# Where the differential attention's weights are scaled and split: in their own stage, or during the first MLP through DRAM

## The chip, the cores and the metric

One core of one Trainium2 chip runs the whole program. The metric is the device time of one execution in microseconds (us), the median of several runs.

## The reference

Two transformer blocks run one after the other on 512 tokens (16 meta tokens are put ahead, 528 columns in all) with a width of 1024. The first has two layers: a stick-breaking attention with a squared-ReLU MLP, and a differential attention with a second such MLP. The second block has a forgetting attention, a gated linear recurrence and a mixture of 32 experts. The change touches the second layer of the first block, cut here to its projections:

```python
h = h + squared_relu_mlp(h, mlp_norm_g[0], mlp_w_in[0], mlp_w_out[0])   # the first MLP
kvn = rmsnorm(h, kv_norm_g)
kv = kvn @ kv_w                                   # 1024 x 2048: keys and values
hn = rmsnorm(h, b_norm_g[j])
qq = (hn @ b_w_q[j])                              # 1024 x 1024: queries
o = differential_attention(q1, q2, k1, k2, vv, lam)
h = h + merge_heads(o) @ b_w_o[j]
h = h + squared_relu_mlp(h, mlp_norm_g[1], mlp_w_in[1], mlp_w_out[1])
```

`rmsnorm` divides by the root of the mean square and multiplies by a vector of gains; everything is float32. Since both norms see the same `h`, the kernel normalizes once and puts each norm's gains into the rows of the weight behind it.

## The kernel before, in words

A dense product is made at nearly float32 precision from three products of float32r: weight and activation are each split into a high part (a copy rounded to float32r) and a low part (the rest), and `product` (L164 on) adds high by high, high by low and low by high over eight blocks of 128 rows (L172 to L174). Weights come in column tiles of 128 x 8 x 128 (512 KB). A column tile is used on two halves of 264 columns, or on the 512 real ones. The result lies in one of two PSUM banks called `dn`, which VectorE evacuates (L202 in an MLP's second product, L367 in its first, L209 for attention's projections).

`sequence` (L76 on) lists all weight tiles of the program in the order in which they are used. `fetch` (L123) has up to NW = 3 raw tiles (`wraw`) on the way, loaded by SP's DMA queue. A tuple with a third entry names a norm: there GpSimd multiplies the raw tile by that norm's gains (L132). `take` (L135) keeps up to two split tiles ahead: ScalarE copies to `whi` (L144), VectorE subtracts to `wlo` (L145). Each of these names has two buffers.

The stages around the change, with the times of the profile:

- The first MLP (about 320 to 690 us), `mlp` (L355). Four rounds c: eight tiles of `mlp_in`, whose results are squared and split (`relu`, `rhi`, `rlo`), then eight tiles of `mlp_out` whose products are added to `h` (`accumulate`). In the last round each tile of `h` is also split for the next stage and stored to DRAM (`hbuf`, L643).
- The differential stage (about 690 to 945 us), `layer_b`. `df_dense` makes for head p the keys (tile `kv[p]`), the queries (`b_q[p]`) and the values (`kv[7 + p]`, one head later): 24 tiles. `head_norm` normalizes each head's keys and queries and rotates them, with a matmul (L703) and a GpSimd multiplication (L708); `stack` and `double` split them (L334, L335, L351 to L353). `df_attn` makes scores (L812), softmax (L825 to L869), transposes (L847), the product with the values (L919) and a norm of the output (L928, L314, L931).
- The output's weights `b_o` follow as raw tiles, then the second MLP with the same `mlp`.

TensorE's order is the program's: `script` steps through `df_attn`, and the tuples PAT, LEAD and END say by hand how many pieces of dense work go between two pieces of attention. The order on the other engines is set by a list scheduler in which evacuations and weight splits have a higher priority (AHEAD_E, AHEAD_W). Every engine works through its own queue in order.

```python
if len(n) > 2 and n[2] is not None:
    g = self.gains[:, n[2] * KT:(n[2] + 1) * KT]
    self.nc.gpsimd.tensor_mul(raw, raw, g[:, :, None].to_broadcast([128, KT, 128]))
```

Of the kernel before, what the change touches and what calls it, by code (L numbers as in the profile page):

```python
# [7 lines left out]
F32 = mybir.dt.float32  # L8
F32R = mybir.dt.float32r
# [8 lines left out]
KT = 8  # L18
# [4 lines left out]
HALVES = ((0, H0), (H0, L))  # L23
# [6 lines left out]
class Net:  # L30
    def __init__(self, ctx, tc, w):
        self.ctx, self.tc, self.nc, self.w = ctx, tc, tc.nc, w
        ctx.enter_context(tc.manual_schedule(engines={mybir.EngineType.PE}))
        self.const = ctx.enter_context(self.phase("const"))
        self.dense_pools = ExitStack()
        pools = self.dense_pools.enter_context
        self.wraw = ctx.enter_context(self.phase("wraw", self.NW, "right"))
        ctx.callback(self.dense_pools.close)
        self.act = pools(self.phase("act", 1, "right"))
        self.wsp = pools(self.phase("wsp", 2, "right"))  # L40
        self.dn = pools(self.banks("dn", 2, "right"))
        self.nc.scalar.preload_act_table_set("natural_log_exp_and_others")
        self.sources, self.rawq, self.splitq = iter(self.sequence()), [], []
        self.fetch(1)
        self.constants()

# [29 lines left out]
    def sequence(self):  # L76
        w = self.w
        for p in range(8):
            for i in range(3):
                yield w["a_qkv"][p, i], KT  # L80
        for k in range(2):
            for t in range(KT):
                yield w["a_o"][t][:, 4 * k:4 * k + 4, :], 4
        for layer in range(2):
            if layer:
                for p in range(9):
                    if p < 8:
                        yield w["kv"][p], KT, 2
                        yield w["b_q"][p], KT, 3
                    if p:  # L90
                        yield w["kv"][7 + p], KT, 2
                for k in range(2):
                    for t in range(KT):
                        yield w["b_o"][t][:, 4 * k:4 * k + 4, :], 4
            for c in range(4):
                for j in range(KT):
                    yield w["mlp_in%d" % layer][c * KT + j], KT
                for j in range(KT):
                    yield w["mlp_out%d" % layer][c, j], KT
        yield w["w2f"][0], KT  # L100
        for p in range(4):
            for c in (0, 4, 8):
                yield w["w2"][c + p], KT
        for h in range(8):
            for c in (20, 28, 12, 36):
                yield w["w2"][c + h], KT
        for t in range(2):
            yield w["w2"][44 + t], KT
            yield w["w2"][52 + t], KT
        for t in range(2):  # L110
            yield w["w_ao"][t], 4
        for t in range(KT):
            yield w["w_ho"][t], KT
            if t < 6:
                yield w["w2"][46 + t], KT
                yield w["w2"][54 + t], KT
                yield w["w_ao"][t + 2], 4
            if t < self.NWO:
                yield w["w_o"][t // 4, t % 4], KT, None, True
        for t in range(self.NWO, KT):  # L120
            yield w["w_o"][t // 4, t % 4], KT, None, True

    def fetch(self, most=8):  # L123
        while len(self.rawq) < min(most, self.NW):
            n = next(self.sources, None)
            if n is None:
                return
            raw = self.wraw.tile([128, KT, 128], F32, name="wraw")[:, :n[1], :]
            self.nc.sync.dma_start(raw, n[0])
            if len(n) > 2 and n[2] is not None:  # L130
                g = self.gains[:, n[2] * KT:(n[2] + 1) * KT]
                self.nc.gpsimd.tensor_mul(raw, raw, g[:, :, None].to_broadcast([128, KT, 128]))  # L132
            self.rawq.append((raw, len(n) > 3))

    def take(self):  # L135

        nc = self.nc
        while len(self.splitq) < 2 and self.rawq and not self.rawq[0][1]:
            raw, _ = self.rawq.pop(0)
            kt = raw.shape[1]  # L140
            hi = self.wsp.tile([128, KT, 128], F32R, name="whi")[:, :kt, :]
            lo = self.wsp.tile([128, KT, 128], F32R, name="wlo")[:, :kt, :]
            with self.tc.high_priority(offset=self.AHEAD_W):
                nc.scalar.activation(hi, raw, AF.Copy)  # L144
                nc.vector.tensor_sub(lo, raw, hi)  # L145
            self.splitq.append((hi, lo))
            self.fetch()
        return self.splitq.pop(0)
# [203 lines left out]
            self.nc.vector.tensor_sub(out[2 + i][r], x[r], out[i][r])  # L352
            self.nc.scalar.activation(out[i][self.ROWS[1 - i]], x[r], AF.Copy)  # L353

    def mlp(self, act, halves, after):  # L355
        nc = self.nc
        with self.phase("mlp") as mp, self.banks("mb", 1) as mb:
            extra = [mb.tile([128, 512], F32, name="mb%d" % i) for i in range(4)]
            for c in range(4):
                r = []  # L360
                for j in range(KT):
                    hi = mp.tile([128, L], F32R, name="rhi", bufs=12)
                    lo = mp.tile([128, L], F32R, name="rlo", bufs=12)

                    def sq(ps, a, b):
                        x = mp.tile([128, 512], F32, name="relu", bufs=3)[:, :b - a]
                        nc.vector.scalar_tensor_tensor(x, ps, 0.0, self.rstd[:, a:b], op0=ALU.max, op1=ALU.mult)  # L367
                        nc.scalar.activation(x, x, AF.Square, scale=0.5)
                        self.split(x, hi[:, a:b], lo[:, a:b])
                    if c == 0 and j < 2:  # L370
                        if j == 0:
                            ps = self.opening(act, halves, extra)
                            self.begin_norm()
                        else:
                            w = self.take()
                            ps = [self.product(w, act, a, b, x[:, :b - a]) for (a, b), x in zip(halves, extra[2:])]
                        for p, (a, b) in zip(ps, halves):
                            with self.tc.high_priority(offset=self.AHEAD_E):
                                sq(p, a, b)
                    else:  # L380
                        for _ in self.dense(act, sq, halves):
                            pass
                    r.append((hi, lo))
                self.accumulate(r, halves, after if c == 3 else None)

# [235 lines left out]
    def layer_a(self):  # L623
        self.hg = self.pair("hg", self.act)
        self.begin_norm()
        self.open_h(self.w["xT"], ALL)
        self.fetch()
        for t in range(KT):
            self.split_tile(t, self.h[:, t, :], [(0, self.hg, ALL)])
        for t in range(KT):  # L630
            self.square_tile(t, self.h[:, t, :])
        with self.phase("sbo") as op:
            o = self.pair("oT", op)
            with self.phase("sb") as self.ap, self.banks("zp", 4) as self.zp, self.banks("op", 1) as self.op:
                self.sb_setup()
                self.ready, self.used, self.outs, self.T, self.when = [], 0, 0, 0.0, []
                self.pace(self.sb_attn(o), self.sb_dense(self.hg2(), self.hg2(o)), self.RATIO_A)
            self.begin_norm()
            self.accumulate(self.hg2(o)[4:], HALVES, lambda t: self.norm_tile(t, self.h[:, t, :], [(1, self.hg, ALL)]))

        def after(t):
            self.norm_tile(t, self.h[:, t, :], [(None, self.hg, ALL)])
            self.nc.sync.dma_start(self.hbuf[:, t, :], self.h[:, t, :])  # L643
        self.mlp(self.hg2(), HALVES, after)
        self.hres.close()

    def hg2(self, pair=None):
# [1363 lines left out]
    PATH = (2, 2, 0, 0, 4, 2, 0, 0, 0, 0, 1, 0, 1)  # L2011

    def run(self):
        dram = self.ctx.enter_context(
            self.tc.tile_pool(name="hbuf", bufs=1, space=bass.MemoryType.DRAM))
        self.vbuf = dram.tile([S, D], F32, name="vbuf")
        self.hbuf, self.hrow = dram.tile([128, KT, L], F32, name="hbuf"), dram.tile([128, 4, D], F32, name="hrow")
        self.layer_a()
        self.layer_b()
        self.mixer()  # L2020
        self.moe()
# [91 lines left out]
```

## Time and profile before

| | |
|---|---|
| median of 3 runs | 2522.99 us (2521.88 to 2525.36) |
| the profiled execution | 2519.31 us |
| its span, first to last instruction | 2517.5 us |
| granted TensorE clock, mean | 0.99 |
| TensorE busy | 2420.2 us, 96% of the span |
| VectorE busy | 1477.1 us, 59% |
| ScalarE busy | 1140.8 us, 45% |
| GpSimd busy | 155.3 us, 6% |

PE is TensorE's matmuls and PEld its weight loads, DVE is VectorE, ACT ScalarE, POOL GpSimd and SP the SyncE, whose queue issues the loads. "L145" is line 145 of the kernel. `out<-in` names the tiles that an instruction writes and reads. A clock of 1.00 is 2.4 GHz, the lower level is 1.2 GHz, and a share between them is a stretch that had both. A wait is put down to the engine whose work came last before the waiting instruction started.

### The profile page before, as it was taken

To read this page: it belongs to the slowest core of one execution; us is meant where nothing else is said; L and a number is where in the kernel's file an instruction comes from. 1 tells how busy PE (TensorE), PEld (TensorE's weight loads), DVE (VectorE), ACT (ScalarE), POOL (GpSimd) and SP (SyncE) were. 2 spreads that over 40 slices of the span, in tenths; PEclk is the share of its full clock that TensorE was granted. 3 is DMA by queue.
4 is the path that set the end of the run, shared out by engine and by line. 5 is a ranking of instruction groups with operands and counts; after the bars stand their busy time and mean duration, and the time that the engine had idled before them with its cause. 6 is when DMAs were issued, how large, how long until landed. Compare 5 with 4: busy or idle time off the path is not lost. (4 is left out here: it accounts for less than half of the span.)

```text
span 2517.5 us, 38128 instructions
## 1 busy us (share of the span) xinstructions
PE 2420.2 (96%) x14656; PEld 1928.4 (77%) x14656; DVE 1477.1 (59%) x2759; ACT 1140.8 (45%) x2166; POOL 155.3 (6%) x126
## 2 busy tenths in 40 slices
PE   8999999999989899999999999999999889999996
PEld 7999999999977777788887988999888633343332
DVE  6666654344589986533445658889654654344434
ACT  7777643233367776422334656655553221121112
POOL 0000000000133220000000000000000310000000
PEclk9999999999999999999999999999999899999998
DMA  3111233332321113333333212222246699997996
GB/s 120 52 53 36 73 94 91 93 93 87 125 69 44 51 34 110 94 99 92 93 100 117 68 59 60 67 61 62 87 131 220 250 408 408 408 397 296 408 408 236
DMA packets 113303, 368.42 MB, mean 146 GB/s; under 512 B 14944, under 2 KB 19296, under 8 KB 113120
## 3 DMA queue, kind: packets, MB, share of 16 engines
q1 hardware_dynamic: 109520, 357.58, 40.9%
q0 software_dynamic: 3024, 6.30, 0.7%
q8 instruction: 116, 1.90, 0.3%
q10 hardware_dynamic: 576, 2.10, 0.2%
q14 instruction: 67, 0.55, 0.1%
HBM read 362.19 MB, written 8.45 MB: 147 GB/s over the span
## 5 line engine op out<-in xcount | busy, mean ns | idle before, releaser
L172 PE MATMUL dn<-hg_hi,whi 128*128 128x264 f32 (+1 forms) x2096 | 676.1, 323 | 8.8 <-ACT hg_hi L293 6.8
L173 PE MATMUL dn<-hg_lo,whi 128*128 128x264 f32 (+1 forms) x2096 | 663.2, 316 | 2.1 <-DVE hg_lo L294 2.0
L174 PE MATMUL dn<-hg_hi,wlo 128*128 128x264 f32 (+1 forms) x2096 | 664.1, 317 | 0.0
L144 ACT ACTIVATE whi<-wraw 128x1024 fp32r<-128x1024 f32 (+1 forms) x285 | 284.9, 1000 | 606.0 <-PE dn L173 529.6
L172 PEld LDWEIGHTS dn<-hg_hi,whi 128*128 128x128 f32 x2096 | 396.8, 189 | 37.7 <-ACT hg_hi L293 6.8
L173 PEld LDWEIGHTS dn<-hg_lo,whi 128*128 128x128 f32 x2096 | 396.7, 189 | 31.1 <-DVE hg_lo L294 4.3
L174 PEld LDWEIGHTS dn<-hg_hi,wlo 128*128 128x128 f32 x2096 | 397.0, 189 | 24.8
L145 DVE TENSOR_TENSOR wlo<-wraw,whi 128x1024 fp32r<-128x1024 f32 (+1 forms) x285 | 332.4, 1166 | 91.8 <-ACT whi L144 90.3
L172 PE MATMUL dn<-rhi,whi 128*128 128x264 f32 (+1 forms) x768 | 247.1, 322 | 2.2 <-DVE h L202 1.7
L174 PE MATMUL dn<-rhi,wlo 128*128 128x264 f32 (+1 forms) x768 | 246.8, 321 | 0.0
L173 PE MATMUL dn<-rlo,whi 128*128 128x264 f32 (+1 forms) x768 | 246.6, 321 | 0.0
L1791 PE MATMUL b<-ew,X 128*64 128x512 f32 (+1 forms) x964 | 235.7, 595 | 3.0 <-DMA ew<-e_in 2.9
L1791 PEld LDWEIGHTS b<-ew,X 128*64 128x64 f32 (+1 forms) x964 | 76.4, 138 | 150.7 <-issue 123.5
L202 DVE TENSOR_TENSOR h<-h,dn 128x264 f32<-128x264 f32 (+1 forms) x120 | 61.7, 514 | 200.3 <-PE dn L174 200.1
L172 PEld LDWEIGHTS dn<-rhi,whi 128*128 128x128 f32 x768 | 144.4, 188 | 14.9 <-DVE h L202 2.9
L173 PEld LDWEIGHTS dn<-rlo,whi 128*128 128x128 f32 x768 | 144.5, 188 | 11.4
L174 PEld LDWEIGHTS dn<-rhi,wlo 128*128 128x128 f32 x768 | 144.5, 188 | 11.1
L1019 DVE SCALAR_TENSOR_TENSOR H<-b,lsg 128x512 f32<-128x512 f32 x17 | 11.7, 691 | 215.8 <-ACT lsg L1018 215.8
L367 DVE SCALAR_TENSOR_TENSOR relu<-dn,rstd 128x264 f32<-128x264 f32 (+1 forms) x93 | 48.2, 519 | 130.3 <-PE dn L174 130.3
L1818 PE MATMUL b<-ew,HT 128*64 128x512 f32 (+1 forms) x476 | 115.0, 599 | 1.8 <-DVE X L1778 1.8
L1016 ACT ACTIVATE lsg<-b 128x512 f32<-128x512 f32 x17 | 10.1, 597 | 225.6 <-PE b L1791 225.6
L1823 ACT ACTIVATE yh<-b,gs 128x512 fp32r<-128x512 f32 x34 | 23.4, 687 | 169.8 <-PE b L1818 169.2
(521 smaller groups left out, 4205.1 us busy)
## 6 DMA issues: line engine op xcount, KB each, us to landing
ew<-e_in SPq DMA_DIRECT2D x233, 512.0 KB, 10.2
ew<-e_out SPq DMA_DIRECT2D x108, 512.0 KB, 10.2
wraw<-mlp_in SPq DMA_DIRECT2D x64, 512.0 KB, 3.6
wraw<-mlp_out SPq DMA_DIRECT2D x64, 512.0 KB, 3.7
wraw<-w SPq DMA_DIRECT2D x60, 512.0 KB, 3.6
wraw<-a_qkv SPq DMA_DIRECT2D x24, 512.0 KB, 3.7
wraw<-e_in SPq DMA_DIRECT2D x23, 512.0 KB, 10.2
wraw<-kv SPq DMA_DIRECT2D x16, 512.0 KB, 3.6
```

Source lines behind the costliest of these rows:

```text
L144: nc.scalar.activation(hi, raw, AF.Copy)
L145: nc.vector.tensor_sub(lo, raw, hi)
L172: nc.tensor.matmul(ps, whi[:, k, :], hi[:, a:b], start=(k == 0), stop=False)
L173: nc.tensor.matmul(ps, whi[:, k, :], lo[:, a:b], start=False, stop=False)
L174: nc.tensor.matmul(ps, wlo[:, k, :], hi[:, a:b], start=False, stop=(k == len(act) - 1))
L202: self.nc.vector.tensor_add(self.h[:, t, a:b], self.h[:, t, a:b], ps)
L367: nc.vector.scalar_tensor_tensor(x, ps, 0.0, self.rstd[:, a:b], op0=ALU.max, op1=ALU.mult)
L1016: nc.scalar.activation(t, x, AF.Abs)
L1019: nc.vector.scalar_tensor_tensor(out, x, 0.0, t, op0=ALU.min, op1=ALU.subtract)
L1791: nc.tensor.matmul(ps[r], X[:, k, r], w[k][:, c:c + 512], start=(k == 0), stop=(k == KT - 1), skip_group_check=True)
L1818: nc.tensor.matmul(ys[c][r], HT[:, k, r], w[k][:, c * 512:c * 512 + 512], start=(k == 0), stop=(k == 3), skip_group_check=True)
L1823: nc.scalar.activation(yh, ys[c], AF.Copy, scale=gate)
```

## The change

For the 24 tiles of `kv` and `b_q`, `sequence` now yields an entry that says that the tile is made ready ahead (`ready_made`), and that has two DRAM tensors of 512 KB each. A generator `make` runs inside the first MLP alone. For each such tile it loads the raw weight over SP's queue, lets GpSimd multiply it by the gains where there are any (all 24 have them), and at the next step splits it on ScalarE and VectorE into `phi` and `plo`, which GpSimd's DMA queue stores to DRAM. One step is taken after each column tile of that MLP, from the third of its first round on; a tile takes two steps. `fetch` loads nothing for such an entry, and `take` loads its two parts from DRAM into `whi` and `wlo` over SP's queue.

```diff
@@ -40,7 +40,9 @@
         self.wsp = pools(self.phase("wsp", 2, "right"))
         self.dn = pools(self.banks("dn", 2, "right"))
         self.nc.scalar.preload_act_table_set("natural_log_exp_and_others")
-        self.sources, self.rawq, self.splitq = iter(self.sequence()), [], []
+        self.dram = ctx.enter_context(tc.tile_pool(name="hbuf", bufs=1, space=bass.MemoryType.DRAM))
+        self.made, self.first = [], 0
+        self.sources, self.rawq, self.splitq = iter(list(self.sequence())), [], []
         self.fetch(1)
         self.constants()
 
@@ -85,10 +87,10 @@
             if layer:
                 for p in range(9):
                     if p < 8:
-                        yield w["kv"][p], KT, 2
-                        yield w["b_q"][p], KT, 3
+                        yield self.ready_made(w["kv"][p], 2)
+                        yield self.ready_made(w["b_q"][p], 3)
                     if p:
-                        yield w["kv"][7 + p], KT, 2
+                        yield self.ready_made(w["kv"][7 + p], 2)
                 for k in range(2):
                     for t in range(KT):
                         yield w["b_o"][t][:, 4 * k:4 * k + 4, :], 4
@@ -120,23 +122,55 @@
         for t in range(self.NWO, KT):
             yield w["w_o"][t // 4, t % 4], KT, None, True
 
+    def ready_made(self, src, gain=None):
+
+        n = len(self.made)
+        self.made.append((src, gain, [self.dram.tile([128, KT, 128], F32, name="pre%s%d" % (x, n)) for x in "hl"]))
+        return None, n
+
+    def make(self, pool):
+
+        nc = self.nc
+        for src, gain, (dh, dl) in self.made[self.first:]:
+            raw = pool.tile([128, KT, 128], F32, name="praw", bufs=2)
+            nc.sync.dma_start(raw, src)
+            if gain is not None:
+                g = self.gains[:, gain * KT:(gain + 1) * KT]
+                nc.gpsimd.tensor_mul(raw, raw, g[:, :, None].to_broadcast([128, KT, 128]))
+            yield
+            hi, lo = (pool.tile([128, KT, 128], F32R, name="p%s" % x, bufs=2) for x in ("hi", "lo"))
+            self.split(raw, hi, lo)
+            nc.gpsimd.dma_start(dh, hi.bitcast(F32))
+            nc.gpsimd.dma_start(dl, lo.bitcast(F32))
+            self.first += 1
+            yield
+
     def fetch(self, most=8):
         while len(self.rawq) < min(most, self.NW):
             n = next(self.sources, None)
             if n is None:
                 return
+            if n[0] is None:
+                self.rawq.append((n[1], None))
+                continue
             raw = self.wraw.tile([128, KT, 128], F32, name="wraw")[:, :n[1], :]
             self.nc.sync.dma_start(raw, n[0])
-            if len(n) > 2 and n[2] is not None:
-                g = self.gains[:, n[2] * KT:(n[2] + 1) * KT]
-                self.nc.gpsimd.tensor_mul(raw, raw, g[:, :, None].to_broadcast([128, KT, 128]))
             self.rawq.append((raw, len(n) > 3))
 
     def take(self):
 
         nc = self.nc
         while len(self.splitq) < 2 and self.rawq and not self.rawq[0][1]:
-            raw, _ = self.rawq.pop(0)
+            raw, kind = self.rawq.pop(0)
+            if kind is None:
+                made = self.made[raw][2]
+                out = []
+                for nm, d in zip(("whi", "wlo"), made):
+                    out.append(self.wsp.tile([128, KT, 128], F32R, name=nm))
+                    nc.sync.dma_start(out[-1].bitcast(F32), d)
+                self.splitq.append(out)
+                self.fetch()
+                continue
             kt = raw.shape[1]
             hi = self.wsp.tile([128, KT, 128], F32R, name="whi")[:, :kt, :]
             lo = self.wsp.tile([128, KT, 128], F32R, name="wlo")[:, :kt, :]
@@ -352,10 +386,11 @@
             self.nc.vector.tensor_sub(out[2 + i][r], x[r], out[i][r])
             self.nc.scalar.activation(out[i][self.ROWS[1 - i]], x[r], AF.Copy)
 
-    def mlp(self, act, halves, after):
+    def mlp(self, act, halves, after, make=()):
         nc = self.nc
         with self.phase("mlp") as mp, self.banks("mb", 1) as mb:
             extra = [mb.tile([128, 512], F32, name="mb%d" % i) for i in range(4)]
+            steps = self.make(mp) if make else iter(())
             for c in range(4):
                 r = []
                 for j in range(KT):
@@ -381,7 +416,14 @@
                         for _ in self.dense(act, sq, halves):
                             pass
                     r.append((hi, lo))
-                self.accumulate(r, halves, after if c == 3 else None)
+                    if c or j > 1:
+                        next(steps, None)
+
+                def then(t):
+                    next(steps, None)
+                    if c == 3:
+                        after(t)
+                self.accumulate(r, halves, then)
 
 
 
@@ -641,7 +683,7 @@
         def after(t):
             self.norm_tile(t, self.h[:, t, :], [(None, self.hg, ALL)])
             self.nc.sync.dma_start(self.hbuf[:, t, :], self.h[:, t, :])
-        self.mlp(self.hg2(), HALVES, after)
+        self.mlp(self.hg2(), HALVES, after, True)
         self.hres.close()
 
     def hg2(self, pair=None):
@@ -2011,8 +2053,7 @@
     PATH = (2, 2, 0, 0, 4, 2, 0, 0, 0, 0, 1, 0, 1)
 
     def run(self):
-        dram = self.ctx.enter_context(
-            self.tc.tile_pool(name="hbuf", bufs=1, space=bass.MemoryType.DRAM))
+        dram = self.dram
         self.vbuf = dram.tile([S, D], F32, name="vbuf")
         self.hbuf, self.hrow = dram.tile([128, KT, L], F32, name="hbuf"), dram.tile([128, 4, D], F32, name="hrow")
         self.layer_a()
```

## Rows read from the trace of the kernel before

**Rows 1.** Busy us, share of the span and instructions, from the page.

```profile
PE 2420.2 (96%) x14656; PEld 1928.4 (77%) x14656; DVE 1477.1 (59%) x2759; ACT 1140.8 (45%) x2166; POOL 155.3 (6%) x126
```

**Rows 2.** Windows, two stages: length, busy PE, PEld, DVE, ACT, POOL, clock, DMA share, GB/s.

```profile
340.00:690.00 350.00, 350.00 (x2871) 349.98 (x2871) 157.68 (x250) 115.02 (x187) 6.73 (x3) 1.00 0.32 96
...
690.00:945.00 255.00, 228.96 (x1412) 195.50 (x1411) 229.58 (x412) 183.73 (x404) 74.82 (x45) 0.97 0.17 50
```

**Rows 3.** Waits of PE in 690 to 990: us in total, times, longest us.

```profile
PE dn L703 <- DVE xf L209: 10.2, 6, 2.1
PE dn L928 <- DVE xf L209: 5.7, 5, 1.3
PE z L812 <- ACT dfq L353: 4.0, 2, 3.7
PE dn L172 <- DVE xf L209: 2.0, 2, 1.7
```

**Rows 4.** Windows of 10 us in the differential stage, columns as in rows 2.

```profile
720.00:730.00 10.00, 5.08 (x22) 4.49 (x23) 9.82 (x15) 5.62 (x13) 4.74 (x3) 0.59 0.19 56
...
850.00:860.00 10.00, 7.88 (x36) 6.50 (x37) 7.93 (x15) 6.53 (x18) 3.18 (x2) 0.83 0.35 105
```

**Rows 5.** Timeline of POOL and DVE, 780 to 788: start us, us, instruction.

```profile
780.22 1.90 POOL L132 TENSOR_TENSOR wraw<-wraw,gains 128x1024 f32<-128x1024 f32 x1 [5.68 <-DMA wraw<-b_q]
...
780.30 2.36 DVE L314 SCALAR_TENSOR_TENSOR ors<-sq,ors 128x512 f32<-128x512 f32 x1
...
783.79 1.20 DVE L145 TENSOR_TENSOR wlo<-wraw,whi 128x1024 fp32r<-128x1024 f32 x1
...
785.73 0.43 DVE L825 TENSOR_REDUCE st<-z 128x2 f32<-128x288 f32 x1
...
787.06 0.17 DVE L839 RECIPROCAL st<-st 128x2 f32<-128x2 f32 x1 [0.70 <-ACT e L836]
...
787.39 0.68 DVE L209 SCALAR_TENSOR_TENSOR xf<-dn,rstd 128x512 f32<-128x512 f32 x1
```

**Rows 6.** By tile, DVE: ns min/median/max over the whole program.

```profile
L314 DVE SCALAR_TENSOR_TENSOR ors<-sq,ors x16: 668/693/2429, 780.3 to 1792.6; 128x512 f32<-128x512 f32 x16
...
L705 DVE SCALAR_TENSOR_TENSOR xf<-xf,bsmall,hrs x16: 729/762/2291, 709.5 to 936.2; 128x528 f32<-128x528 f32 x8, 128x512 f32<-128x512 f32 x8
...
L145 DVE TENSOR_TENSOR wlo<-wraw,whi x285: 680/1224/2912, 5.6 to 1911.5; 128x1024 fp32r<-128x1024 f32 x120, 128x512 fp32r<-128x512 f32 x23
```

**Rows 7.** Windows, one engine alone: DVE writing `wlo`, then POOL's L132: busy (count).

```profile
690.00:945.00 255.00, 32.02 (x24) 0.97 0.17 50
...
690.00:945.00 255.00, 45.95 (x21) 0.97 0.17 50
```

**Rows 8.** Timeline of DVE in the first MLP, 441 to 446.

```profile
441.11 0.43 DVE L367 SCALAR_TENSOR_TENSOR relu<-dn,rstd 128x264 f32<-128x264 f32 x1 [0.39 <-PE dn L174]
...
444.06 0.43 DVE L367 SCALAR_TENSOR_TENSOR relu<-dn,rstd 128x264 f32<-128x264 f32 x1 [1.13 <-PE dn L174]
445.03 1.23 DVE L145 TENSOR_TENSOR wlo<-wraw,whi 128x1024 fp32r<-128x1024 f32 x1 [0.54 <-ACT whi L144]
```

**Rows 9.** DMA issues (count, KB each, us to landing), and a GpSimd issue in ns.

```profile
wraw<-a_o SPq DMA_DIRECT2D x16, 256.0 KB, 2.6
...
wraw<-kv SPq DMA_DIRECT2D x16, 512.0 KB, 3.6
...
L1464 POOL DMA_DIRECT2D vbuf<-vrow x4: 588/590/783, 1959.1 to 1992.4; - x4
```

**Rows 10.** Timeline of PE: a tile's last high product; start of the tile after next.

```profile
696.77 0.29 PE L172 MATMUL dn<-hg_hi,whi 128*128 128x264 f32 x1
...
702.69 0.29 PE L172 MATMUL dn<-hg_hi,whi 128*128 128x264 f32 x1
...
770.44 0.28 PE L172 MATMUL dn<-hg_hi,whi 128*128 128x264 f32 x1
...
778.28 0.40 PE L172 MATMUL dn<-hg_hi,whi 128*128 128x512 f32 x1
```

## The prediction

> **What bounds the kernel now.** First the page's busy times [rows 1]: TensorE is busy for 96% of the span, so a change pays only where TensorE stands still or runs at the lower clock. Next the busy times of two stages [rows 2]. In the first MLP (340 to 690 us) TensorE is busy for all of 350 us, VectorE for 158, ScalarE for 115 and GpSimd for 7: those three have room. In the differential stage (690 to 945) TensorE is busy for 229.0 of 255 us, VectorE for 229.6 (90%), ScalarE for 183.7, and the granted clock is 0.97. So TensorE stands for 26.0 us there, and the clock costs about 229 x 0.03 = 7 us more: 33 us is the most that this stage can give.
>
> Then TensorE's waits around that stage [rows 3]: 10.2 + 5.7 + 2.0 = 17.9 us for VectorE's evacuation of a projection (L209; TensorE has two `dn` banks for these), and 4.0 us for ScalarE's L353, 3.7 of it at once. That leaves 26.0 - 17.9 - 4.0 = 4.1 us of small waits. The 10 us windows [rows 4] show the clock: 0.59 in 720 to 730, where TensorE was busy for 5.08 of 10 us, and 0.83 in 850 to 860, where it was busy for 7.88.
>
> Why VectorE is late is seen in one head [rows 5]. The evacuation at 787.39 stands behind L839, which waited for ScalarE's exponentials, and those for the maximum L825 (785.73). Ahead of L825 are a weight split of 1.20 us (783.79) and an L314 of 2.36 us (780.30) that began 0.08 us after a GpSimd multiplication. That L314 has a median of 0.69 us, and the same holds elsewhere: L705 has 0.76 us and at most 2.29, the split L145 1.22 and at most 2.91 [rows 6]. A VectorE operation with two SBUF inputs can be held up to 1.7 us while GpSimd multiplies; the evacuations from PSUM are not (L209 keeps its 0.43 us under an L132).
>
> **The change part by part.** For each of 24 weight tiles it removes from the differential stage one GpSimd multiplication, one ScalarE copy and one VectorE subtraction. In 690 to 945 us these are 45.95 us of GpSimd and 32.0 of VectorE [rows 7]. 21 of the 24 multiplications lie there, and three of its 24 splits are of `b_o` and stay, so VectorE loses 21 x 1.33 = 28 us. It also loses the holding: on its timeline I counted 17 operations that overlap an L132, from 699.26 to 894.65 us, with 23 us above their line's usual time; the L314 of rows 5 is one. VectorE falls from 229.6 to about 179 us.
>
> Term 1, the 17.9 us. In rows 5, 1.20 + (2.36 - 0.69) = 2.9 us go from ahead of an evacuation for which TensorE waited 2.1 us, the longest of its kind [rows 3]. The other kind (L928, up to 1.3 us) has a held L705 before it. What is late next: L708's multiplications stay and still hold L869, and ScalarE's exponentials are in the same chain. Bounds 0 and 17.9; I take 80%, 14 us.
>
> Term 2, the 4.0 us at the start and the 4.1 of small waits. The first head's queries come through VectorE and ScalarE, which both lose splits there, but the chain of small steps stays. Bounds 0 and 8.1; I take half, 4.
>
> Term 3, the clock. It was low in windows in which TensorE stood [rows 4]; with fewer waits some of the 7 us come back. Bounds 0 and 7; I take 3.
>
> Term 4, what the first MLP pays. Each tile adds a load, a multiplication of about 2 us, a ScalarE copy, a subtraction of 1.22, and two stores issued by GpSimd at 0.59 us [rows 9]. A step follows each column tile, one per 2 x 2.95 = 5.9 us (two evacuations, 441.11 and 444.06 [rows 8]), and a tile takes two of the 62, so 48 steps do it, long before the first ready tile is loaded. VectorE gets 21 x 1.22 = 26 us and at most 24 x 1.7 of holding: 158 becomes at most 225 of 350. An evacuation has those 2.95 us until TensorE wants its bank again; behind a new subtraction it ends 1.2 us later. The weight's split ends at 446.3 (445.03 + 1.23 [rows 8]) and is needed at 444.06 + 5.9 = 449.9. GpSimd works 2 + 2 x 0.59 us in a period of 11.8, and a tile's load and multiplication are issued a step before its split, so that ScalarE's in-order queue, with the next weight's copy behind, should not wait. On SP the new loads stand between raw weights that are fetched three tiles ahead. Three multiplications already ran in this MLP's tail and TensorE did not wait. The worst that I can build with one hold is 1.7 + 1.22 + 0.43 against 2.95 us, 0.4 a tile: bounds 0 and 10. I take 2, near the tail's zero.
>
> Term 5, the loads. A ready tile is two 512 KB loads, which SP issues when TensorE has finished the tile before the last: less lead than the raw weights had. 256 KB lands in 2.6 us and 512 KB in 3.6 [rows 9], so 1 us for 256 KB more, and I estimate 5.6 us for both. From a tile's last high product to the start of the tile after the next there are 702.69 - 697.06 = 5.6 us at the stage's start and 778.28 - 770.72 = 7.6 later [rows 10]; the others that I read are up to 23 us. So the loads lie beside TensorE's work, but for the start. On SP's queue behind them are only `rope` and two small loads, at the start, and `b_o`, later. If the cover goes, each of 8 heads pays what exceeds 7.6 us. Bounds 0 and 8; I take 1. The Trainium skill (DMA: Bandwidth & Descriptors, Anatomy of one DMA) fits a transfer by 2.0 us plus its bytes at 436 GB/s; worked out from that page, an estimate, the pair lands in 4.4 us, this term is 0 and the sum 1 us better.
>
> The second MLP runs the same code without steps. Later stages start earlier by what is won, their loads with them.
>
> The sum is 14 + 4 + 3 - 2 - 1 = 18 us. The profiled execution took 2519.3 us, 3.7 below the median of 2523.0; from the median, 2505 us.
>
> **The rivals.** *Nearly all comes back*: terms 1 to 3 at their ends, less 2, are 31 us: 2492. For it: VectorE falls to three quarters. Against it: with TensorE earlier, ScalarE's chains (184 us) are late next.
>
> *The ready parts come late.* If a pair needs over 7.6 us, TensorE waits for a DMA in VectorE's place, some 1 us in each of 8 heads and 2 at the start: of 18 us 10 are lost, 2515. Against it: 3.6 us for one such load [rows 9].
>
> *The wait only moves.* TensorE's order is written by hand; if ScalarE's chains end the same waits, all terms give some 2 us and the MLP takes them: 2523.
>
> *Slower: the evacuations of the first MLP.* Place: VectorE's queue in 340 to 600 us. If a weight split held to 2.91 us and a new subtraction of 1.22 both stand ahead of an evacuation of 0.43, that is 4.56 against 2.95 us. TensorE then waits 1.6 us for each of 24 tiles, 38 us, and the sum is 2505 + 36 = 2541. It decides from 0.8 us a tile on. For it: TensorE has no slack in that MLP. Against it: a new subtraction comes after its own multiplication, so both rarely fall on one evacuation. The Trainium skill (SBUF — State Buffer, SBUF: two separate sides) says that GpSimd and a VectorE operation with two SBUF inputs exclude each other for a whole instruction; the trace agrees (2.36 us for 0.69 [rows 5, 6]), and this rival is that rule in a stage that had hardly any GpSimd work.
>
> **How the numbers follow.** Chances: the forecast (18 us, give or take 7) 0.55, nearly all 0.13, late loads 0.12, the moved wait 0.11, slower 0.09. A measurement of this kernel can tell about 0.2%, 5 us, from no change. Faster by more are the first three, 0.80; within it the fourth, 0.11; slower 0.09. The likeliest gives 2505. The range is from 2490 (all terms at their good ends) to 2523, the moved wait; the slower case and little more lies outside.
>
> **What would show it.** In the changed profile: no L132 work in 690 to 945 us and VectorE near 180 us there; TensorE's waits for L209 under 5 us; a granted clock over 0.98; the first MLP with TensorE still busy throughout; hardly a wait for a load of `whi` or `wlo`. I am wrong if waits for L209 stay above 10 us, if ScalarE or a load takes their place, or if the first MLP grows by more than 5 us.

## The result and the profile after

The changed kernel takes 2538.6 us (2534.9 to 2542.8, 5 runs) against 2523.7 us (2521.9 to 2525.4, 5 runs): a ratio of 1.0059, 95% interval 1.0047 to 1.0072. It is 15 us slower; I had forecast 18 us faster, and the time lies outside my range.

Two marks in SP's queue part the span: the last store of `h` at the end of the first MLP (`hbuf<-h`) and the last load of it after the differential stage (`h<-hbuf`). In the kernel before they were issued at 690.3 and 989.8 us. Here are the rows of the kernel before and of the changed one (first and last start at the end of a row):

```profile
L643 SPq DMA_DIRECT2D hbuf<-h x8: 326/326/327, 649.1 to 690.3; - x8
L621 SPq DMA_DIRECT2D h<-hbuf x8: 326/430/432, 986.6 to 989.8; - x8
...
L685 SPq DMA_DIRECT2D hbuf<-h x8: 320/327/330, 687.1 to 728.2; - x8
L663 SPq DMA_DIRECT2D h<-hbuf x8: 327/430/440, 1000.9 to 1004.1; - x8
```

From mark to mark there are 275.9 us in place of 299.5: the differential stage wins 23.6 us. But the first mark comes 37.9 us later. The windows say where (columns as in [rows 2]; the last row is of the kernel before):

```profile
340.00:728.00 388.00, 365.80 (x2908) 363.48 (x2908) 192.55 (x274) 136.12 (x211) 67.69 (x68) 0.97 0.52 171
728.00:960.00 232.00, 222.83 (x1410) 192.82 (x1409) 172.34 (x390) 165.16 (x381) 26.36 (x16) 0.99 0.31 110
330.00:460.00 130.00, 103.21 (x751) 100.50 (x750) 79.24 (x87) 50.33 (x69) 69.45 (x66) 0.91 0.91 324
460.00:728.00 268.00, 268.00 (x2200) 268.00 (x2200) 119.70 (x195) 90.06 (x149) 4.01 (x9) 1.00 0.34 102
...
330.00:460.00 130.00, 130.00 (x1067) 130.00 (x1067) 57.07 (x95) 45.56 (x78) 0.00 (x0) 1.00 0.31 91
```

The differential stage (second row) answers to [rows 2]: VectorE has 172 us of work in place of 230, the clock is 0.99, and TensorE stands for 9.2 us in place of 26. The loss is all in the third row, 330 to 460 us: TensorE is busy for 103 of 130 us, at a clock of 0.91, with 324 GB/s of transfers. It gets 751 matmuls done there; the kernel before did 1067. After 460 us TensorE is busy throughout again. The waits of TensorE around that stretch (300 to 480 us, columns as in [rows 3]):

```profile
PE dn L206 <- DVE h L236: 14.8, 3, 5.1
PE dn L206 <- DVE relu L402: 10.5, 7, 3.4
PE dn L207 <- DVE rlo L360: 1.4, 1, 1.4
```

These 26.7 us and about 103 x 0.09 = 9 us for the clock make 36 of the 37.9. Both main rows are evacuations, so VectorE is late, and it is not out of time (79 of 130 us). Its timeline at the longest wait, with what each instruction stood idle for:

```profile
386.83 0.43 DVE L236 TENSOR_TENSOR h<-h,dn 128x264 f32<-128x264 f32 x1 [0.43 <-PE dn L208]
391.98 1.22 DVE L360 TENSOR_TENSOR plo<-praw,phi 128x1024 fp32r<-128x1024 f32 x1 [4.72 <-ACT phi L359]
396.07 1.23 DVE L360 TENSOR_TENSOR plo<-praw,phi 128x1024 fp32r<-128x1024 f32 x1 [2.87 <-ACT phi L359]
397.21 0.42 DVE L236 TENSOR_TENSOR h<-h,dn 128x264 f32<-128x264 f32 x1
```

And the queues behind it, GpSimd's, ScalarE's and the loads in SP's:

```profile
388.96 1.89 POOL L139 TENSOR_TENSOR praw<-praw,gains 128x1024 f32<-128x1024 f32 x1 [3.09 <-DMA praw<-b_q]
392.87 2.08 POOL L139 TENSOR_TENSOR praw<-praw,gains 128x1024 f32<-128x1024 f32 x1 [2.02 <-DMA praw<-kv]
...
390.88 1.06 ACT L359 ACTIVATE phi<-praw 128x1024 fp32r<-128x1024 f32 x1 [6.13 <-POOL praw L139]
394.98 1.06 ACT L359 ACTIVATE phi<-praw 128x1024 fp32r<-128x1024 f32 x1 [3.04 <-POOL praw L139]
...
382.90 0.33 SPq L136 DMA_DIRECT2D praw<-b_q  x1
384.96 0.33 SPq L136 DMA_DIRECT2D praw<-kv  x1
```

The evacuation at 397.21 stands in VectorE's queue behind two subtractions of the making; the first stood idle for a ScalarE copy, that for a GpSimd multiplication, that for a load. The loads were slow: from issue to the multiplication that waited for them it took 6.1 us (382.90 to 388.96) and 7.9 (384.96 to 392.87), where 3.6 is usual in the kernel before [rows 9]. VectorE did nothing for 4.7 and then 2.9 us. The matmuls for the evacuation at 397.21 ended at about 389.7, half of a column tile's 5.85 us after those for the one at 386.83 (an estimate), so for some 5 of these 7.6 us it was ready behind. Over the whole stretch (315 to 465 us) VectorE stood idle for 35 us ahead of subtractions of the making, not all of it with an evacuation ready:

```profile
DVE plo L360 <- ACT phi L359: 30.2, 10, 4.7
...
DVE plo L360 <- DMA prel<-plo: 4.8, 1, 4.8
```

How dense the making is comes from the row of its subtraction (ns min/median/max, first and last start):

```profile
L360 DVE TENSOR_TENSOR plo<-praw,phi x24: 1208/1226/2921, 321.0 to 458.1; 128x1024 fp32r<-128x1024 f32 x24
```

and from the MLP's own weight splits (L179 alone, one per column tile), in a window from the first subtraction to the end of the last:

```profile
321.00:458.20 137.20, 27.66 (x17) 0.91 0.90 320
```

All 24 tiles were made in 137 us, 5.7 us each, beside 17 column tiles; by the prediction's 48 steps, one per 5.9 us, it would have been some 280 us, beside 48.

### The profile page after: what moved, and what is told of

It reads as the page before. It is cut to its first block, busy times and chain, and to the rows that moved or that the text cites. A ratio compares the mean times of both kernels' runs of the same rounds, so it can differ in the third digit from the quotient of the medians.

```text
span 2533.1 us, 38349 instructions
## 1 busy us (share of the span) xinstructions
PE 2424.8 (96%) x14656; PEld 1933.9 (76%) x14656; DVE 1458.0 (58%) x2759; ACT 1143.8 (45%) x2166; POOL 179.5 (7%) x174
## 5 line engine op out<-in xcount | busy, mean ns | idle before, releaser
L178 ACT ACTIVATE whi<-wraw 128x1024 fp32r<-128x1024 f32 (+1 forms) x261 | 259.2, 993 | 566.1 <-PE dn L207 493.8
L179 DVE TENSOR_TENSOR wlo<-wraw,whi 128x1024 fp32r<-128x1024 f32 (+1 forms) x261 | 304.9, 1168 | 77.4 <-ACT whi L178 75.7
L206 PEld LDWEIGHTS dn<-rhi,whi 128*128 128x128 f32 x768 | 146.6, 191 | 25.5 <-DVE h L236 13.1
L1058 ACT ACTIVATE lsg<-b 128x512 f32<-128x512 f32 x17 | 10.1, 597 | 225.2 <-PE b L1833 225.2
```

The source lines that it names most:

```text
L206: nc.tensor.matmul(ps, whi[:, k, :], hi[:, a:b], start=(k == 0), stop=False)
L1058: nc.scalar.activation(t, x, AF.Abs)
```

## The experiments

Two lengths are compared in all of them. The first MLP is counted from the start of its first L367 (`relu`; 324.8 us before, 324.9 in the changed kernel) to the last store of `h`: 365.5 us before, 403.3 after, a loss of 37.8. The differential stretch runs from that store to the last load of `h`: 299.5 and 275.9. The lengths are read from one profiled execution of each kernel. The tied kernel, the first of them, was run four times and each of the others once; the kernel before took 2523.9 to 2528.6 us in the seven runs beside the first four experiments, 2524.2 and 2523.7 beside the later ones.

**The making tied to TensorE's progress.** Each tile's gains pass through a copy of eight columns that reads a result of the present column tile (the lines that set `self.tie` to `h` in the MLP's second product are alike):

```diff
-                nc.gpsimd.tensor_mul(raw, raw, g[:, :, None].to_broadcast([128, KT, 128]))
+                pg = pool.tile([128, KT], F32, name="pg", bufs=2)
+                nc.vector.scalar_tensor_tensor(pg, self.tie, 0.0, g, op0=ALU.mult, op1=ALU.add)
+                nc.gpsimd.tensor_mul(raw, raw, pg[:, :, None].to_broadcast([128, KT, 128]))
...
                     if c or j > 1:
+                        self.tie = hi[:, :KT].bitcast(F32)
                         next(steps, None)
```

> Theory A (density): the making of the 24 tiles is not tied to TensorE's progress, so its instructions stand back to back in the queues of VectorE and ScalarE, waiting for loads and multiplications with the MLP's evacuations behind them; here each tile's gains pass through a small VectorE copy that reads a result of the present column tile, so that a tile is made per two column tiles. A expects the first MLP to end (last hbuf store) within 5 us of 690, against 728 in the changed kernel, with making spread over some 280 us, and about 2500 us in all (2523.7 less the 23.6 that the differential stage wins). Theory B (the work itself): the copies, subtractions, held operations and stores cost about 1.6 us a tile wherever they stand; it expects an end near 728 again and about 2538 us. Theory C (transfers saturated at 330 GB/s make the loads late) expects an end below 705 too, since the same bytes are spread over twice the time: runs without stores tell it from A.

Measured: 2498.2 us (2497.0 to 2500.0, 4 runs) against 2524.7, a ratio of 0.989 (0.9873 to 0.9906). Its subtractions, by their tile:

```profile
L362 DVE TENSOR_TENSOR plo<-praw,phi x24: 1224/1225/1227, 337.6 to 606.9; 128x1024 fp32r<-128x1024 f32 x24
```

The weight splits in that window, then the MLP's window with all engines as in [rows 2]:

```profile
337.60:607.00 269.40, 56.30 (x46) 1.00 0.67 223
...
340.00:690.00 350.00, 349.99 (x2870) 349.79 (x2869) 180.41 (x299) 135.59 (x212) 73.24 (x77) 1.00 0.61 199
```

The same work, spread over 269 us, costs the MLP 0.2 us (365.7), and TensorE does not stand there. The differential stretch is 275.7. So the work itself has room there, as I had reckoned, and theory B falls. This version beats both kernels.

**Making alone.** `ready_made` yields the raw weight again and `fetch` multiplies as before; the stored parts are not read.

```diff
-        return None, n
+        return src, KT, gain
```

> The tiles are made and stored during the first MLP as in the changed kernel, but the differential stage loads, scales and splits the raw weights as before and never reads the stored parts. If the two halves of the change are independent: the MLP ends near 728, the stretch from there to the last load of h keeps its 299.5 us, and the time is about 2523.7 + 37.9 = 2561 us. If the MLP's loss came from the way ready tiles are fetched, the MLP would end near 690 and the time be about 2524.

Measured: 2562.0 us; the MLP takes 401.0, the differential stretch 300.7. The two halves of the change are independent: 35.5 us lost here, 23.6 won there. How the ready tiles are fetched has hardly a part in the loss (37.8 with it, 35.5 without).

**Making without stores.** As the last one, and the two stores of each tile are left out.

```diff
-            nc.gpsimd.dma_start(dh, hi.bitcast(F32))
-            nc.gpsimd.dma_start(dl, lo.bitcast(F32))
```

> As the run that only makes, but the two parts are not stored (they are not read either). Theory C (saturated transfers): with 25 MB less in that stretch the loads come in time and the MLP ends below 700. Theory A (density, queues in order): the making is still back to back, GpSimd's multiplication and the split still take some 4 us a tile in a row, and the MLP ends between 705 and 725; a part of the loss goes because nothing waits for stores to free the two buffers of each part. Theory B: 720 or more.

Measured: 2550.7 us; the MLP takes 392.8 us, so 27.3 of the loss remain. TensorE's waits (300 to 730 us):

```profile
PE dn L207 <- DVE h L237: 8.8, 5, 2.0
PE dn L207 <- DVE relu L403: 8.6, 6, 2.6
```

and the weight splits beside the making, with the rate of transfers at the end of the row:

```profile
324.30:431.80 107.50, 23.84 (x14) 0.93 0.56 172
```

At 172 GB/s the DMA engines are busy for 56%, where they were for 90%, and the evacuations still wait; the last store of `h` comes at 721.0, where theory A had it and theory C had not. So saturated transfers (theory C) are not needed for the loss, though the stores make the chain slower (5.7 us a tile with them, 107.5 / 24 = 4.5 without) and add some 10 us to it.

**No multiplication.** The gains are left out of the making, so `kv` and `b_q` are unscaled; the rest is the changed kernel.

```diff
-                nc.gpsimd.tensor_mul(raw, raw, g[:, :, None].to_broadcast([128, KT, 128]))
```

> The changed kernel without the multiplication by the gains (so kv and b_q are unscaled): GpSimd only issues stores. Theory D (GpSimd's multiplications hold VectorE and lengthen the chain) expects the MLP to end below 700. Theory C expects it near 728, as the bytes are the same. Theory A expects between 705 and 728: the chain is 2 us shorter per tile but still back to back.

Measured: 2539.5 us; the MLP takes 401.4 us. The subtractions now wait for the stores too (VectorE's waits, 315 to 465 us):

```profile
DVE plo L357 <- DMA prel<-plo: 26.7, 9, 4.4
DVE plo L357 <- ACT phi L356: 13.8, 9, 2.8
```

and the transfers run at 385 GB/s beside 12 column tiles:

```profile
323.30:432.70 109.40, 14.61 (x12) 0.91 1.00 385
```

The loss is 35.9 us without the multiplication, so it needs neither that link of the chain nor what the multiplication holds, and theory D falls. But another link has taken its place, the stores, with the DMA engines busy all the time (1.00); that the multiplication had no part in the changed kernel's own loss is not shown, and the weight splits there did take 27.66 / 17 = 1.63 us in place of 1.22 [rows 8]. My expectation's upper end for theory A (728) was passed by 2.6 us of the mark, and theory C had expected this end: the run does not part the two. The run without stores did, and the next one does.

**Tied and dense.** The tied version with two steps at each column tile, in both places where a step is taken.

```diff
-                        next(steps, None)
+                        next(steps, None), next(steps, None)
```

> The tied making, but with two steps at each column tile instead of one: a tile is made per column tile of 5.9 us, about the rate at which the changed kernel really made them (24 in 140 us), yet never ordered ahead of TensorE's progress. If the loss comes from the order (two subtractions of the making planned per column tile, which the chip can't keep up with, so that evacuations stand behind them), the first MLP ends below 705 and the time is 2500 to 2512. If the rate as such costs it (VectorE, GpSimd and transfers at 320 GB/s in one stretch), it ends near 728 and the time is near 2535.

Measured: 2507.3 us; the MLP takes 374.2 us, a loss of 8.7. TensorE's waits (300 to 690 us):

```profile
PE dn L208 <- DVE relu L404: 4.0, 9, 0.5
PE dn L208 <- DVE h L238: 0.9, 1, 0.9
```

and the splits beside the making:

```profile
335.10:478.90 143.80, 54.23 (x24) 1.00 0.95 330
```

As many tiles in nearly as short a time, at 330 GB/s, and a quarter of the loss: no wait exceeds 0.9 us. The rate as such is not what cost 38 us; an order free to run ahead of TensorE was. The 24 weight splits took 54.23 / 24 = 2.26 us each here, against 1.22 in the kernel before [rows 8]: nearly all were held beside a multiplication, and still the MLP pays only 8.7 us.

**One buffer.** The changed kernel, untied, with `bufs=1` for `praw`, `phi` and `plo`.

```diff
-            raw = pool.tile([128, KT, 128], F32, name="praw", bufs=2)
+            raw = pool.tile([128, KT, 128], F32, name="praw", bufs=1)
```

> The changed kernel, untied, with one buffer instead of two for the raw weight and for each part, so that the order on VectorE's queue has one subtraction of the making per column tile instead of two. By the order theory (the planned rate exceeds what the chip makes) the loss of 38 us in the first MLP shrinks to less than half, an end below 710; if being untied is what costs, whatever the planned rate, or if one buffer makes each tile's chain later still, it ends at 728 or above.

Measured: 2553.8 us; the MLP takes 421.7 us, a loss of 56.2. My expectation, less than half the loss, missed. VectorE's and ScalarE's longest waits in 315 to 520 us:

```profile
DVE plo L360 <- ACT phi L359: 88.4, 21, 6.4
...
ACT phi L359 <- POOL praw L139: 103.5, 22, 7.4
```

and the splits beside the making:

```profile
323.50:538.00 214.50, 34.47 (x27) 0.94 0.69 236
```

More column tiles stand between the makings, 27 for 24, but a tile now takes 8.9 us (214.5 / 24). Both sides of the comparison moved, and only their difference counts. A column tile takes 5.85 us undisturbed (48 of the 2871 matmuls in 350 us of [rows 2]). If TensorE must pass N column tiles while the making takes T, the loss is T - 5.85 N:

| kernel | T, us | N | T - 5.85 N | loss of the MLP, us |
|---|---|---|---|---|
| changed | 137.2 | 17 | 37.8 | 37.8 |
| making alone | 135.9 | 17 | 36.5 | 35.5 |
| no stores, making alone | 107.5 | 14 | 25.6 | 27.3 |
| no multiplication | 109.4 | 12 | 39.2 | 35.9 |
| one buffer | 214.5 | 27 | 56.6 | 56.2 |
| tied, dense | 143.8 | 24 | 3.4 | 8.7 |
| tied | 269.4 | 46 | 0.3 | 0.2 |

Six of the seven agree within 4 us, less than one column tile; the dense one has 5 us more, beside short waits, nine of them of up to 0.5 us. Since T and N are both read from the run, the table only says that the loss lies in the stretch of the making. That TensorE is held there to the pace of the making is read from the timeline above and from the two tied runs: N is set by the order in VectorE's queue, T by how fast loads, multiplications, copies and stores come.

**Scaled only.** The next three runs ask which part of the change won the 24 us. Tied making, but only the scaled weight is stored; the differential stage splits it.

```diff
-            self.split(raw, hi, lo)
-            nc.gpsimd.dma_start(dh, hi.bitcast(F32))
-            nc.gpsimd.dma_start(dl, lo.bitcast(F32))
+            nc.gpsimd.dma_start(dh, raw)
```

> Tied making, but only the scaled weight is stored, unsplit; the differential stage loads it as a raw tile and splits it there, without GpSimd's multiplication. This parts the 24 us that the differential stage won (299.5 to 275.7 us from the last store of h to its last load) into the multiplications with what they hold (23 us of VectorE by my count) and the splits (28 us). If each counts by VectorE's time, about 24 x 23/51 = 11 us stay won: 289 us, 2511 in all. If the held operations alone made the waits, 278 us; if the splits alone, 297.

Measured: 2504.8 us; the stretch is 279.7. TensorE's waits (693 to 950 us) answer to [rows 3]:

```profile
PE dn L746 <- DVE xf L242: 4.3, 6, 1.0
PE z L855 <- ACT dfq L386: 3.2, 2, 2.7
...
PE dn L205 <- DVE xf L242: 0.9, 1, 0.9
```

Without the multiplications 19.8 of the 23.8 us are won, and the splits are worth the other 4. I had expected 11 us to stay won if each counted by VectorE's time, and 21.5 if the held operations alone made the waits; 19.8 is near the second.

**Memsets, and an idle multiplication.** Beside each load of a scaled weight GpSimd does work that nothing needs: two memsets of a scratch tile, or a multiplication of the weight into it.

```diff
+                self.nc.scalar.activation(self.junk[:, 0, :1], raw[:, 0, :1], AF.Copy)
+                for _ in range(2):
+                    self.nc.gpsimd.memset(self.junk, 0.0)
```

```diff
+                self.nc.gpsimd.tensor_mul(self.junk, raw, g[:, :, None].to_broadcast([128, KT, 128]))
```

> The run that stores scaled weights unsplit (279.7 us from the last store of h to its last load, 299.5 in the kernel before), and beside each such load two GpSimd memsets of 0.95 us on a scratch tile, started by a one-column ScalarE copy of the weight, so that GpSimd is as busy as with the multiplication but reads nothing. If the multiplications cost by holding VectorE's operations with two SBUF inputs, the stretch stays at 280 to 283 us. If they cost by keeping GpSimd's queue busy before L708, it goes back to 290 or more.

> The same kernel with a GpSimd multiplication of the loaded weight by the gains into a scratch tile that nothing reads, in place of the memsets. If holding VectorE is the cost, the stretch goes back to 294 to 300 us although no split waits for the result. If the cost was that the splits had to wait for the multiplication, it stays at 280 to 284.

Measured: 2515.0 and 2523.5 us; the stretches are 292.1 and 303.2 us. TensorE's waits with the memsets:

```profile
PE dn L210 <- ACT ms L344: 7.0, 5, 2.0
PE dn L751 <- DVE xf L247: 4.6, 6, 0.9
```

and with the idle multiplication:

```profile
PE dn L750 <- DVE xf L246: 10.1, 6, 2.1
PE dn L975 <- DVE xf L246: 5.0, 5, 1.1
PE z L859 <- ACT dfq L390: 3.6, 2, 3.1
PE dn L209 <- DVE xf L246: 2.7, 2, 2.4
```

The idle multiplication brings back [rows 3] almost number for number, though no split waits for it. The run with memsets missed its expectation (280 to 283 us) and doesn't settle its question by the time: a wait for ScalarE (7.0 us) came up, probably since the one-column copies, for which ScalarE stood 10.1 us until loads landed, are in ScalarE's queue; that was not tried apart. VectorE's late evacuations stay at 4.6 us there. What settles it is VectorE's busy time from mark to mark, for scaled only, memsets and the idle multiplication (columns as in [rows 2]):

```profile
693.50:973.20 279.70, 264.01 (x1601) 221.80 (x1599) 228.30 (x463) 214.62 (x469) 25.52 (x16) 0.99 0.18 57
...
689.90:982.00 292.10, 269.47 (x1600) 226.03 (x1598) 228.91 (x462) 217.54 (x489) 68.71 (x66) 0.98 0.17 54
...
690.30:993.50 303.20, 274.49 (x1600) 230.09 (x1598) 257.85 (x462) 214.28 (x469) 77.45 (x45) 0.96 0.16 52
```

The same VectorE work takes 228.3, 228.9 and 257.9 us. The memsets, which raise GpSimd's busy time from 25.5 to 68.7 us, lengthen it by 0.6 us; the multiplications, which read a weight, by 29.6. So what cost was the holding of VectorE.

## Why the prediction was wrong

**The step that failed is term 4**, "what the first MLP pays": I took 2 us of 0 to 10, and it was 37.8. Its sentence "A step follows each column tile, one per 2 x 2.95 = 5.9 us" took the place of a step in the text for its place in time. Only TensorE's order is the program's. On the other engines nothing tied a making to a column tile but its own two buffers, so the scheduler ran it ahead: the first subtraction started at 321.0 us, before the MLP's first evacuation (324.9), though in the text it stands behind the fourth column tile, and 24 makings came beside 17 column tiles, which the chip could not keep up with. "ScalarE's in-order queue, with the next weight's copy behind, should not wait" then fell as well: ScalarE waited for up to 6.1 us, VectorE for 4.7 behind it. The amounts in term 4 were within its bounds: in the tied run VectorE is busy for 180 us of the MLP's 350, below my bound of 225, and the MLP pays 0.2 us.

**The slower rival had the place and nearly the number, by another mechanism.** I gave it 0.09 and 2541 us, 1.6 us a tile in VectorE's queue of the first MLP; it was 37.8 / 24 = 1.6 a tile. But its price was a held weight split plus a new subtraction, and without any multiplication (no holding) the loss was nearly the same, 35.9 us. In the tied dense run, where held splits and new subtractions do stand side by side, the MLP pays 8.7 us, 0.4 a tile. What stood ahead of the evacuation at the longest wait was, after it was ready, some 5 us of idle time and two subtractions of 1.2, none of them held. That the rival's number came so near is luck.

**Terms 1 to 3 and 5 held in sum.** Together they gave 14 + 4 + 3 - 1 = 20 us, measured 23.6. TensorE stands for 9.2 us where it stood for 26.0, 16.9 less (terms 1 and 2 gave 18), and its busy time for nearly the same matmuls fell by 6.1 us (228.96 to 222.83), which term 3 had at 3. In the changed kernel's differential stage (728 to 960 us) TensorE waits for the projections' evacuation once, for 2.0 us:

```profile
PE dn L745 <- ACT ms L340: 3.4, 7, 0.5
PE o L961 <- DVE wT L894: 2.2, 6, 0.4
PE dn L745 <- DVE xf L243: 2.0, 1, 2.0
PE z L854 <- ACT dfq L387: 1.1, 2, 0.7
```

So term 1 was 15.9 (I took 14 of 17.9). The start's wait of 4.0 became 1.1, but small waits came in its place, the largest for ScalarE (3.4 us), which I had named as late next: of term 2's 4 us about 1 was won (16.9 - 15.9). The clock went from 0.97 to 0.99. No wait for a load of `whi` or `wlo` is among TensorE's rows, so term 5 is about 0. Where the landing was recorded, in the tied run, the second part landed 4.1 us after its own issue, and it was issued some 0.4 to 0.5 us behind the first: the pair took about 4.6 us, an estimate. My 5.6 was too long. The 4.4 us worked out from the Trainium skill (DMA: Bandwidth & Descriptors, Anatomy of one DMA), also an estimate, is nearer, though that section gives its fit for DMAs issued by GpSimd and these were issued by SP:

```profile
whi<-preh SPq DMA_DIRECT2D x24, 512.0 KB, 3.2
wlo<-prel SPq DMA_DIRECT2D x24, 512.0 KB, 4.1
```

**What of the win belongs to which part was not foreseen.** The prediction gave VectorE 28 us back from the splits and 23 from the holding and parted term 1 no further. The runs give about 4 us of the win to the splits and 20 to the multiplications. The reading that fits, not tried apart, is that a short operation on the way to an evacuation, stretched from 0.69 to 2.36 us, delays TensorE, and a split with two tiles of lead mostly does not.

What I named as proof of error, "if the first MLP grows by more than 5 us", is what happened.

## What to carry to other kernels

Work moved into a stage with idle engines is hidden only if its order in their queues can't outrun what the chip delivers: one instruction that waits for a late input stops everything behind it, and an engine that is 60% busy can still be late. Compare the planned spacing with the chain's own period (load, multiply, copy, subtract, store), and tie the extra work to the critical engine's progress by a small data dependency; here that turned a loss of 15 us into a gain of 26. When a GpSimd operation runs beside a latency-bound chain on VectorE, price what it holds and not only what it computes.

## What the hardware showed that was not expected

A GpSimd multiplication whose result nobody reads cost the differential stretch 23.5 us (303.2 against 279.7). The Trainium skill (SBUF — State Buffer, SBUF: two separate sides) has a VectorE operation with two SBUF inputs and a GpSimd operation that reads SBUF exclude each other, and not one that only writes it. The trace agrees: the same VectorE work took 257.9 us beside the multiplications and 228.9 beside the memsets. With the multiplications TensorE's waits for VectorE's projections are 17.8 us (10.1 + 5.0 + 2.7), without them 5.2 (4.3 + 0.9). What I had not expected is that most of these waits hang on the holding and so little on the splits.
